# Sums of a Strassen product's weight quarters: accumulating DMAs that read SBUF in place of HBM, with other buffer counts and another place for a part of the adaLN sums

## The chip, the cores and the metric

The kernel runs on one core of a Trainium2 chip. The metric is device time in microseconds (us) of one execution; lower is better. The kernel before takes 841.71 us, the median of 3 runs (840.68 to 843.01).

## What is computed

A trunk of two layers on 512 tokens of width 1024, in float32. In each layer:

```
mod = silu(c) @ w_ada + b_ada                # shift, scale, gate: the three adaLN thirds
h   = rms_norm(x) * (1 + scale) + shift
x_rg, z_rg, x_ml, z_ml, o = split(h @ w_in)  # five parts of 1024 columns
y_rg = rglru(conv(x_rg)) * silu(z_rg)        # gates by block-diagonal products, then a scan over tokens
y_ml = mlstm(x_ml, o) * silu(z_ml)           # 4 heads of 256, in chunks of 128 tokens
x   = x + gate * (concat(y_rg, y_ml) @ w_out)
```

Then a last RMS norm. What the change touches is the part of `h @ w_in` that gives `o` and `z_ml`, called **oz** here, and the adaLN sums.

## The kernel before

**Precision.** A float32 product is done as three matmuls of a rounded format: each operand is split into a high and a low part, and TensorE adds high*high, low*high and high*low (`mm3`, recorded at L154). A weight tile comes in by one DMA of 512 KB into a buffer of the kind `raw`; ScalarE (ACT) casts it to `whi` (L184) and VectorE (DVE) forms `wlo = raw - whi` (L191). That pair of instructions is called a split here. A pair stays until the last matmul that reads it; the raw buffer is free once both have read it, unless somebody else still wants it.

**The planner.** The program is first recorded by a planner, as operations with an engine, a guessed cost, and the tiles they read and write. The planner then fixes the order of each engine's instructions, with due times counted from TensorE's order, and gives every tile a numbered buffer of its kind's pool (`kinds`). Engines run their lists in order and wait for one another by semaphores. So buffer counts and guessed costs change the order everywhere, also in stages that the source does not touch. Loads are issued by SP (L233); an accumulating DMA (`out += source`) is issued by GpSimd (POOL, L241), and is one of the instructions that it issues in order.

**Stages of a layer.** Layer 0: the start and the norm; the mLSTM heads' inputs, to 150 us; the oz stage, from 150 to 238; the RG-LRU stage, from 238 to 341; the out product (two passes, out and outq), from 341. Layer 1's oz stage begins at 537, its RG-LRU stage at 642, and its out product at 744. Boundaries overlap, since the planner mixes neighbours.

**oz.** For a head, `ml_oz` (L1006 on) computes o and z for 512 tokens by a Strassen-like scheme of 7 products in place of 8. Activations are cut in quarters (two halves of the width, two halves of the tokens), and the head's weights in quarters q0, q1, q2, q3 (width half by the columns of o or z), each 512 KB. The products, with the activation quarter or sum of quarters and the weight that they use:

| product | activations | weights |
|---|---|---|
| h11 | quarter | q0 |
| s1 | sum | q0 + q1 |
| s2 | sum | q0 + q1 + q3 |
| h12 | quarter | q2 |
| s3 | sum | q1 + q3 |
| h22 | quarter | q0 + q1 + q3 + q2 |
| s4 | sum | q3 |

Each product is 24 matmuls of 256 columns (4 pieces of width, 2 of tokens, 3 of precision). The weight sums grow in place: one raw buffer `ta` holds q0, is split for h11, gets q1 added by a DMA, is split for s1, gets q3, is split for s2, gets q2, is split for h22. A second one, `tb`, holds q1 and gets q3 for s3. An addition to `ta` can start only when the split before it has read the buffer. Before the change every addition reads its quarter from HBM, and s4 and h12 load theirs plainly: four plain loads and four accumulating ones in a head, 512 KB each.

Around a head's products stand, on TensorE, those of the attention part (`ml_sw`, `ml_sv`, `ml_yt`); its outputs are named `num`, `Mbc`, `yT`. `mrs` is a small power (an inverse root) on GpSimd that `ml_yt` needs; `vh` are small memsets there.

**adaLN sums.** `mod_units` yields one unit at a time: a load of 512 KB of `w_ada2` into a raw buffer by SP, and two DVE operations that multiply by silu(c) and add into `macc` (L199; the first pair at L208). A third is 8 units. A layer's loop has a generator `bg` of 24 units in layer 0 and 8 in layer 1 (`MODAT`). `step_mod(bg, n)` takes n of them. Before, two are taken in each of the four heads, and the rest, two per step, in the out product, which uses the gate third first.

**RG-LRU stage.** `rg_x`, `rg_gates`, `rg_z` are products of 512 columns (rgx, pa, px, rgz), with many DVE operations on their results (`rconv`, `ti`, `tr`, `om`, `rzt`).

Of the kernel before, what the change touches and what calls it, by code (L numbers as in the profile page):

```python
# [15 lines left out]
ALU = mybir.AluOpType  # L16
# [92 lines left out]
class Planner:  # L109
# [128 lines left out]

    def qdma(self, out, in_, nbytes):

        self.op("POOL", lambda: self.nc.gpsimd.dma_start(out.ap(), in_, accum_op=ALU.add), [out], [out], 1.0,  # L241
                tail=nbytes)

    def lat(self, a, b):
        if a != b:
# [191 lines left out]
def trunk_kernel(ctx: ExitStack, tc: tile.TileContext, x, cT, params, bif, bgate, fg,  # L437
# [6 lines left out]
    def pools(name, n, **kw):  # L444
        return n, [ctx.enter_context(tc.tile_pool(name=f"{name}{i}", bufs=1, **kw)) for i in range(n)]

    kinds = {
        "heap": pools("heap", 66),
        "raw": pools("raw", 4),
        "whi": pools("whi", 5),  # L450
        "wlo": pools("wlo", 4),
        "gate": pools("gate", 1),
        "gpart": pools("gpart", 2),
# [8 lines left out]
    def slot(name, dt=F32, shape=(128, 512)):  # L462
        return P.tile("heap", shape, dt, name)

    def bank(name, shape=(128, 512)):
        return P.tile("ps", shape, F32, name)
# [29 lines left out]
    def load_w(src, shape, raw=None, pieces=1):  # L496
        raw = raw or load_raw(src, shape, pieces)
        hi = P.tile("whi", (128,) + shape, F32R, "whi")
        lo = P.tile("wlo", (128,) + shape, F32R, "wlo")
        n = shape[0] // pieces  # L500
        for k in range(0, shape[0], n):
            split(hi[:, k:k + n], lo[:, k:k + n], raw[:, k:k + n])
        return hi, lo

    def mm3(ps, lh, ll, rh, rl, start, stop):
        P.mm(ps, lh, rh, start, False)
        P.mm(ps, lh, rl, False, False)
        P.mm(ps, ll, rh, False, stop)
# [172 lines left out]
    def step_mod(bg, n):  # L681
        for _ in range(n):
            next(bg, None)
# [80 lines left out]
    def chan_group(l, g, hT, names):  # L764
        ps = [bank(n) for n in names]
        for kh in range(2):
            u = w_in_unit(l, g, kh)
            for cc in range(2):
                for k in range(4):
                    chan_mm(ps[cc], u, hT, kh, k, cc, ALLT, kh == 0 and k == 0, kh == 1 and k == 3)  # L770
        return ps
# [10 lines left out]
    def silu2(ps, name, shape=(128, 512)):  # L782

        th = slot(name + "t", F32, shape)
        P.act(th, ps, AF.Tanh, scale=0.5)
        P.stt(th, th, 1.0, ps, ALU.add, ALU.mult)
        return th
# [208 lines left out]
    def ml_oz(l, h, hT, st):  # L996

        src = w_oz[l, h].rearrange("u p (k w n) -> p u k w n", k=2, w=2)  # L1000
        q = [src[:, :, k, w, :] for k in range(2) for w in range(2)]
        form = [[(hT[2 * p + k][0][:, ts], hT[2 * p + k][1][:, ts]) for p in range(4)]
                for k, ts in ((0, slice(0, 256)), (1, slice(0, 256)), (1, slice(256, 512)))]
        h11, h12, h22 = form
        s1, s2, s3, s4 = [[st["sf"][p][n] for p in range(4)] for n in range(4)]

        def parts(raw):
            return load_w(None, (4, 256), raw)

        def quarter(src):  # L1010
            raw = P.tile("raw", (128, 4, 256), F32, "raw")
            P.dma(raw, src, 1 << 19)
            return raw

        def add(raw, src):
            P.qdma(raw, src, 1 << 19)

        def product(f, w):
            ps = bank("oz", (128, 2, 256))
            for b in range(2):  # L1020
                bs = slice(128 * b, 128 * b + 128)
                for k in range(4):
                    mm3(ps[:, b, :], f[k][0][:, bs], f[k][1][:, bs], w[0][:, k, :], w[1][:, k, :],
                        b == 0 and k == 0, b == 1 and k == 3)
            return ps

        def wide(name):
            return slot(name, F32, (128, 2, 256))

        ta = quarter(q[0])  # L1030
        ps = product(h11, parts(ta))
        p1 = wide("ozp")
        P.acopy(p1, ps)
        add(ta, q[1])
        p5 = product(s1, parts(ta))
        c12, c22 = wide("ozc"), wide("ozc")
        P.acopy(c22, p5)
        add(ta, q[3])
        ps = product(s2, parts(ta))
        u = wide("ozu")  # L1040
        P.tt(u, ps, p1, ALU.add)
        P.tt(c12, c22, u, ALU.subtract)
        ps = product(h12, parts(quarter(q[2])))
        o = [wide("oz") for _ in range(2)]
        z = [wide("oz") for _ in range(2)]
        P.tt(p1, ps, p1, ALU.add)
        P.act(o[0], p1, AF.Tanh, scale=0.5)
        yield
        tb = quarter(q[1])
        add(tb, q[3])  # L1050
        ps = product(s3, parts(tb))
        P.tt(u, ps, u, ALU.add)
        P.tt(c22, c22, u, ALU.subtract)
        add(ta, q[2])
        ps = product(h22, parts(ta))
        P.tt(u, ps, u, ALU.add)
        P.act(o[1], u, AF.Tanh, scale=0.5)
        ps = product(s4, parts(quarter(q[3])))
        P.tt(c12, ps, c12, ALU.add)
        for n, c in ((1, c22), (0, c12)):  # L1060
            P.act(z[n], c, AF.Tanh, scale=0.5)
            P.stt(z[n], z[n], 1.0, c, ALU.add, ALU.mult)
        st["oz"][h] = (o, z)
        yield
# [85 lines left out]
    def rg_gates(l, g, st):  # L1150
        if g % 2 == 0:
            st["wr"] = load_w(w_rg[l, g // 2], (4, 2, 128))
            st["om"] = [slot("om") for _ in range(4)]
        wr, om = st["wr"], st["om"]
        for cc in range(2):
            r = 2 * g + cc
            n = r % 4
            xr, hi, lo = st["xr"].pop(r)
            pa, px = bank("pa"), bank("px")
            mm3(pa, wr[0][:, n, 0, :], wr[1][:, n, 0, :], hi, lo, True, True)  # L1160
            mm3(px, wr[0][:, n, 1, :], wr[1][:, n, 1, :], hi, lo, True, True)


            tr, q = slot("tr"), slot("q")
            P.ts(q, pa, par[:, l, P_BA + r:P_BA + r + 1], ALU.add, 0.0, ALU.min)
            P.act(tr, pa, AF.Tanh, scale=0.5, bias=hb[:, l, r:r + 1])
            P.act(q, q, AF.Exp)
            P.act(tr, tr, AF.Abs)
            P.stt(tr, tr, 1.0, q, ALU.add, ALU.mult)
            P.act(q, tr, AF.Exp, scale=hsp[:, l, r:r + 1])  # L1170
            P.act(q, q, AF.Square)
            P.act(tr, tr, AF.Tanh, scale=sp4[:, l, r:r + 1])
            P.act(om[n], q, AF.Square)
            P.stt(om[n], om[n], 1.0, tr, ALU.add, ALU.mult)
            ti = slot("ti")
            P.act(ti, px, AF.Tanh, scale=0.5, bias=hb[:, l, 8 + r:9 + r])
            P.stt(ti, ti, 1.0, xr, ALU.add, ALU.mult)
            st["ai"][r] = (q, ti)

    def rg_z(l, g, hT, st):  # L1180
        pz = chan_group(l, 4 + g, hT, ("rgz0", "rgz1"))
        for cc in range(2):
            st["rz"][2 * g + cc] = silu2(pz[cc], "rz")

    def rg_tail(l, bt, st):
        om = st["om"]
        P.slack = SL_TAIL
        for n in range(4):
            P.act(om[n], om[n], AF.Sqrt, extra=0.7)
        for n in range(4):  # L1190
            r = 4 * bt + n
            a, u = st["ai"].pop(r)
            P.tt(u, u, om[n], ALU.mult)
            P.scan(u, a, u, ALU.mult, ALU.add)
            P.tt(u, u, st["rz"].pop(r), ALU.mult)
            hi, lo = slot("yh", F32R), slot("yl", F32R)
            split_scaled(hi, lo, u, 0.25)
            st["y"][r] = (hi, lo)
        P.slack = SL
# [85 lines left out]
    for l in range(L):  # L1285
# [68 lines left out]
        bg = itertools.chain(*[mod_units(*j) for j in MODAT[l]])  # L1354
        for h in range(NH):
            oz = ml_oz(l, h, hT, st)
            next(oz)
            step_mod(bg, 1)
            if h:
                ml_sv(l, h - 1, st)  # L1360
            else:
                next(gates)
                ml_sw(0, st)
            next(oz)
            step_mod(bg, 1)
            if h + 1 < NH:
                ml_sw(h + 1, st)
            if h:
                ml_yt(l, h - 1, st)
# [3 lines left out]
        ml_yt(l, 3, st)  # L1373
        rg_gates(l, 0, st)
        rg_z(l, 0, hT, st)
        rg_gates(l, 1, st)
        rg_z(l, 1, hT, st)
        rg_tail(l, 0, st)
        rg_x(l, 2, hT, st)
        rg_x(l, 3, hT, st)  # L1380
        rg_gates(l, 2, st)
        rg_z(l, 2, hT, st)
        rg_gates(l, 3, st)
        rg_z(l, 3, hT, st)
        rg_tail(l, 1, st)
        xt = load_x(x if l == 0 else x1d)
        def during_first(u):
# [105 lines left out]
```

## Time and profile before

| what | us |
|---|---|
| median of 3 runs | 841.71 |
| lowest, highest | 840.68, 843.01 |
| the profiled execution's own time | 843.48 |
| its span in the profile | 841.8 |
| granted TensorE clock, mean | 0.99 |

The profile names the engines PE (TensorE matmul), PEld (its weight load), DVE (VectorE), ACT (ScalarE), POOL (GpSimd) and SP. A `q` behind a name is the engine's sequencer, or its DMA issues. L154 and so on are lines of the kernel before. In a row `raw<-in_w_oz_dram`, the tile is written from an input in HBM; numbers in tile names (`raw_2843`) count the recorded tiles, and differ between the two programs. A window row gives for each engine busy time and, in brackets, the count of instructions that began in it. The queue q0 (software_dynamic) holds the accumulating DMAs alone, and q1 the plain ones. A wait row says which engine waited, at which output, for whom, and for how long in all, how many times, and the longest. The chain follows the last instruction back to what released it.

### The profile page before, as it was taken

Reading aid. Unit: us, or ns where it says so; the run is one execution under the profiler, and the core shown is the slowest. Engines: PE = TensorE matmul, PEld = TensorE weight load, DVE = VectorE, ACT = ScalarE, POOL = GpSimd, SP = SyncE. Lnnn points to the kernel's source line nnn. Section 1 sums busy time; section 2 is a strip of 40 time slices with the busy share of each in tenths; the row PEclk is TensorE's granted clock in tenths of the full one; section 3 lists DMA queues with packets and bytes.
Section 4 is the critical chain, followed back from the end, with each engine's and each line's share of the span. In section 5 each row is a group of like instructions: output and inputs, shape, how many; then the busy total and the mean of one; then the engine's idle time right before and its main releaser. Section 6 shows DMA issues by size and latency. Waiting matters only on the chain.

```text
span 841.8 us, 14032 instructions
## 1 busy us (share of the span) xinstructions
PE 814.7 (97%) x5222; PEld 724.9 (86%) x5222; DVE 679.6 (81%) x1339; ACT 530.0 (63%) x1045; POOL 80.4 (10%) x96
## 2 busy tenths in 40 slices
PE   4999999998899999999999999999989999999996
PEld 3778899998888888889999789999988888888996
DVE  5598957897999899788569887589999988976552
ACT  4378755765667879921347667657676687894222
POOL 3000012222011000000010001212120100000000
PEclk9999999998999999999999999999999999999999
DMA  9933346867753414668632443467984442373202
GB/s 317 355 140 125 77 93 132 177 143 170 189 157 120 138 62 147 216 218 269 212 95 101 151 115 61 76 153 174 225 181 146 148 127 76 100 250 100 76 1 100
DMA packets 66243, 124.46 MB, mean 148 GB/s; under 512 B 4864, under 2 KB 39680, under 8 KB 66176
## 3 DMA queue, kind: packets, MB, share of 16 engines
q1 hardware_dynamic: 49280, 106.80, 38.4%
q0 software_dynamic: 16896, 16.78, 13.3%
q8 instruction: 41, 0.67, 0.3%
q14 instruction: 26, 0.21, 0.1%
HBM read 119.36 MB, written 4.19 MB: 147 GB/s over the span
## 4 chain that ended last, share of the span: by engine, by line
PE 85%; DVE 5%; DMA 4%; issue 2%; ACT 2%; POOL 0%; SPq 0%; POOLq 0%; DVEq 0%; ACTq 0%
PE oz L154 12%; PE mx L154 11%; PE rgx L154 11%; PE out L154 11%; PE rgz L154 11%; PE outq L154 10%; PE S L154 3%; DMA raw<-in_w_oz_dram 3%; PE v L154 3%; PE p L154 2%; PE num L154 2%; PE A L154 2%; DVE wlo L191 2%; PE px L154 1%; PE pa L154 1%
## 5 line engine op out<-in xcount | busy, mean ns | idle before, releaser
L184 ACT CAST whi<-raw 128x1024 fp32r<-128x1024 f32 (+1 forms) x157 | 156.5, 1007 | 121.0 <-DMA raw<-in_w_out_dram 35.0
L191 DVE TENSOR_TENSOR wlo<-raw,whi 128x1024 fp32r<-128x1024 f32 (+1 forms) x157 | 180.7, 1160 | 45.6 <-PE outq L154 12.0
L154 PE MATMUL oz<-whi,sh 128*128 128x256 f32 x256 | 74.4, 291 | 4.9 <-ACT ozp L184 3.6
L154 PE MATMUL oz<-wlo,sh 128*128 128x256 f32 x256 | 73.9, 289 | 0.7 <-DVE wlo L191 0.7
L154 PE MATMUL oz<-whi,sl 128*128 128x256 f32 x256 | 73.7, 288 | 0.0
L154 PE MATMUL outq<-whi,yh 128*128 128x256 f32 x256 | 71.4, 283 | 0.0
L154 PE MATMUL outq<-wlo,yh 128*128 128x256 f32 x256 | 71.4, 283 | 0.0
L154 PE MATMUL outq<-whi,yl 128*128 128x256 f32 x256 | 71.3, 282 | 0.0
L241 POOL DMA_DIRECT2D raw<-in_w_oz_dram x32 | 41.4, 1337 | 296.2 <-DVE wlo L191 93.9
L154 PE MATMUL mx<-hh,whi 128*128 128x512 f32 (+1 forms) x166 | 59.5, 359 | 2.1 <-ACT whi L184 2.1
L154 PE MATMUL mx<-hl,whi 128*128 128x512 f32 (+1 forms) x166 | 58.4, 352 | 0.1
L154 PE MATMUL oz<-wlo,hh 128*128 128x256 f32 x192 | 55.2, 288 | 2.7 <-DVE wlo L191 2.7
L154 PE MATMUL mx<-hh,wlo 128*128 128x512 f32 (+1 forms) x166 | 57.5, 349 | 0.0
L154 PE MATMUL oz<-whi,hh 128*128 128x256 f32 x192 | 55.3, 288 | 0.0
L154 PEld LDWEIGHTS oz<-whi,sh 128*128 128x128 f32 x256 | 50.1, 196 | 5.6 <-ACT ozp L184 4.1
L154 PE MATMUL oz<-whi,hl 128*128 128x256 f32 x192 | 54.8, 286 | 0.0
L154 PEld LDWEIGHTS oz<-wlo,sh 128*128 128x128 f32 x256 | 50.0, 195 | 1.0 <-DVE wlo L191 0.9
L154 PE MATMUL rgx<-hl,whi 128*128 128x512 f32 x128 | 50.8, 397 | 0.0
L154 PE MATMUL rgx<-hh,whi 128*128 128x512 f32 x128 | 50.7, 396 | 0.0
L154 PE MATMUL rgx<-hh,wlo 128*128 128x512 f32 x128 | 50.5, 395 | 0.0
L154 PE MATMUL out<-whi,yh 128*128 128x512 f32 x128 | 50.5, 395 | 0.0
L154 PE MATMUL rgz<-hh,whi 128*128 128x512 f32 x128 | 50.5, 394 | 0.0
(279 smaller groups left out, 2460.6 us busy)
## 6 DMA issues: line engine op xcount, KB each, us to landing
raw<-in_w_in_dram SPq DMA_DIRECT2D x45, 512.0 KB, 3.5
raw<-in_w_oz_dram SPq DMA_DIRECT2D x32, 512.0 KB, 4.7
raw<-in_w_oz_dram POOLq DMA_DIRECT2D x32, 512.0 KB, 6.1
raw<-in_w_ada_dram SPq DMA_DIRECT2D x32, 512.0 KB, 4.4
raw<-in_w_out_dram SPq DMA_DIRECT2D x32, 512.0 KB, 4.1
wada<-in_w_adb_dram SPq DMA_DIRECT2D x24, 256.0 KB, 5.3
x<-in_x_dram SPq DMA_DIRECT2D x16, 256.0 KB, 5.4
raw<-in_w_qk_dram SPq DMA_DIRECT2D x8, 512.0 KB, 3.5
```

The costliest lines, as they stand in the source:

```text
L154: self.nc.tensor.matmul(out.ap(), lhsT=lhsT.ap(), rhs=rhs.ap(), start=start, stop=stop, **kw)
L184: self.op("ACT", lambda: self.nc.scalar.copy(out.ap(), in_.ap()), [out], [in_], 0.1 + 0.00084 * in_.n)
L191: self.op(eng, lambda: e.tensor_tensor(out=out.ap(), in0=a.ap(), in1=b.ap(), op=op), [out], [a, b], c)
L241: self.op("POOL", lambda: self.nc.gpsimd.dma_start(out.ap(), in_, accum_op=ALU.add), [out], [out], 1.0, tail=nbytes)
```

## The change

In `ml_oz`, each quarter is loaded once by SP and stays in its raw buffer: `ta` (q0), `tb` (q1), `td` (q3), `tc` (q2). The four additions of a head become SBUF to SBUF: ta += tb, ta += td, tb += td, ta += tc. So a head has four plain loads as before, and four accumulating DMAs that no longer read HBM. The source of an addition is now a tile, and so an input that the planner must keep, and wait for; the planner's guess for such an instruction goes from 1.0 to 1.3. For two raw buffers more there is one whi less and two heap buffers less. The eight units of the adaLN sums that stood in the heads now stand in the RG-LRU stage, two behind each `rg_z`.

```diff
@@ qdma @@
-        self.op("POOL", lambda: self.nc.gpsimd.dma_start(out.ap(), in_, accum_op=ALU.add), [out], [out], 1.0,
-                tail=nbytes)
+        self.op("POOL", lambda: self.nc.gpsimd.dma_start(out.ap(), in_.ap(), accum_op=ALU.add), [out], [out, in_],
+                1.3, tail=nbytes)
@@ kinds @@
-        "heap": pools("heap", 66),
-        "raw": pools("raw", 4),
-        "whi": pools("whi", 5),
+        "heap": pools("heap", 64),
+        "raw": pools("raw", 6),
+        "whi": pools("whi", 4),
         "wlo": pools("wlo", 4),
@@ ml_oz @@
-        add(ta, q[1])
+        tb = quarter(q[1])
+        add(ta, tb)
         p5 = product(s1, parts(ta))
...
-        add(ta, q[3])
+        td = quarter(q[3])
+        add(ta, td)
         ps = product(s2, parts(ta))
...
-        ps = product(h12, parts(quarter(q[2])))
+        tc = quarter(q[2])
+        ps = product(h12, parts(tc))
...
-        tb = quarter(q[1])
-        add(tb, q[3])
+        add(tb, td)
         ps = product(s3, parts(tb))
...
-        add(ta, q[2])
+        add(ta, tc)
         ps = product(h22, parts(ta))
...
-        ps = product(s4, parts(quarter(q[3])))
+        ps = product(s4, parts(td))
@@ the loop over heads, and the RG-LRU stage behind it @@
             next(oz)
-            step_mod(bg, 1)
...
             next(oz)
-            step_mod(bg, 1)
...
         rg_z(l, 0, hT, st)
+        step_mod(bg, 2)
         rg_gates(l, 1, st)
         rg_z(l, 1, hT, st)
+        step_mod(bg, 2)
...
         rg_z(l, 2, hT, st)
+        step_mod(bg, 2)
         rg_gates(l, 3, st)
         rg_z(l, 3, hT, st)
+        step_mod(bg, 2)
```

How the instructions then stand, at two places. First GpSimd's list for the additions of layer 0's fourth head. Before, `raw_2843` is its ta and `raw_3041` its tb:

```order
L241 DMA raw_2843<-in_w_oz_dram 128x4x256 [waits DMAHW5_49,DMAHW7_49,DMAHW2_49,DVE_49]
L241 DMA raw_3041<-in_w_oz_dram 128x4x256 [waits DMAHW4_49,DMAHW7_49,DMASW2_49,DVE_49]
L241 DMA raw_2843<-in_w_oz_dram 128x4x256 [waits DMASW4_49,DVE_49]
L191 TENSOR_TENSOR mrs_3157<-mms_3134,mhalf_429 128x2 [waits DVE_49]
L191 TENSOR_TENSOR mrs_3173<-mms_3137,mhalf_429 128x2 [waits DVE_49]
L1096 MEMSET vh_3211 128x2x2
L1096 MEMSET vh_3234 128x2x2 [waits DVE_49,PE_49]
L241 DMA raw_2843<-in_w_oz_dram 128x4x256 [waits DMASW6_49,DVE_49]
```

And after, where `raw_2580` is ta, `raw_2622` tb, `raw_2933` td and `raw_2964` tc:

```order
L241 DMA raw_2580<-raw_2622 128x1024 [waits DMAHW1_49,DMAHW2_49,DMASW5_49,DVE_49]
L241 DMA raw_2622<-raw_2933 128x1024 [waits DMAHW3_49,DMASW7_49,DMASW4_49]
L241 DMA raw_2580<-raw_2933 128x1024 [waits DVE_49]
L191 TENSOR_TENSOR mrs_3111<-mms_3085,mhalf_426 128x2 [waits DVE_49]
L191 TENSOR_TENSOR mrs_3126<-mms_3097,mhalf_426 128x2 [waits DVE_49]
L1098 MEMSET vh_3165 128x2x2 [waits PE_49,Activation_49]
L1098 MEMSET vh_3202 128x2x2 [waits DVE_49]
L241 DMA raw_2580<-raw_2964 128x1024 [waits DMAHW4_49,DMASW6_49,DVE_49]
```

The order of the four is the same. What changed are the sources, the shape of a transfer (rows of 1024 elements in place of four pieces of 256), and the waits: the second addition, to tb, now waits for the first one too, which reads tb (`DMASW` is an accumulating DMA, `DMAHW` a plain one).

Second, VectorE's list in layer 0's RG-LRU stage. Before:

```order
L191 TENSOR_TENSOR wlo_4042<-raw_3943,whi_4031 128x1024
L199 SCALAR_TENSOR_TENSOR ti_4045<-ti_4045,rconv_3840 128x512
L199 SCALAR_TENSOR_TENSOR tr_3972<-tr_3972,q_3989 128x512
L199 SCALAR_TENSOR_TENSOR tr_4038<-tr_4038,q_4016 128x512
L199 SCALAR_TENSOR_TENSOR rzt_4078<-rzt_4078,rgz0_3991 128x512
L191 TENSOR_TENSOR wlo_4090<-raw_3951,whi_4059 128x1024
```

And after, about the same place:

```order
L191 TENSOR_TENSOR wlo_4044<-raw_3769,whi_4027 128x1024
L191 TENSOR_TENSOR ti_3846<-ti_3846,rzt_3921 128x512
L199 SCALAR_TENSOR_TENSOR macc_3904<-raw_4012,csil_562,macc_3904 128x512
L199 SCALAR_TENSOR_TENSOR om_4052<-om_4052,tr_3975 128x512
L199 SCALAR_TENSOR_TENSOR macc_3916<-raw_4012,csil_562,macc_3916 128x512
L199 SCALAR_TENSOR_TENSOR om_4068<-om_4068,tr_3970 128x512
L191 TENSOR_TENSOR wlo_4086<-raw_3780,whi_4074 128x1024
```

The two sums of a unit (`macc`) now stand between the splits and the RG-LRU's own operations. On SP, the adaLN loads are gone from between the loads of oz and stand among those of the RG-LRU stage.

## The prediction

> **What bounds the kernel now.** I read the page's busy times and chain first, then windows over the stages, then TensorE's waits, the chain and the DMA inside the windows that lose time.
>
> The page's span, its busy times and the chain by engine:
>
> ```profile
> span 841.8 us, 14032 instructions
> PE 814.7 (97%) x5222; PEld 724.9 (86%) x5222; DVE 679.6 (81%) x1339; ACT 530.0 (63%) x1045; POOL 80.4 (10%) x96
> PE 85%; DVE 5%; DMA 4%; issue 2%; ACT 2%; POOL 0%; SPq 0%; POOLq 0%; DVEq 0%; ACTq 0%
> ```
>
> TensorE (PE) is the bound: 97% busy, and 85% of the chain. A change in DMAs can win only what PE loses, by waiting or by running at a lower granted clock. Windows over the oz stages of layer 0 (150 to 238) and layer 1 (from 537) show where that is; the columns are length, busy time with instructions of PE, PEld, DVE, ACT and POOL, granted clock, DMA share and GB/s:
>
> ```profile
> 150.00:180.00 30.00, 30.00 (x251) 29.70 (x250) 27.83 (x62) 22.81 (x54) 6.16 (x7) 1.00 0.80 171
> 180.00:198.00 18.00, 14.40 (x107) 14.13 (x106) 14.96 (x26) 12.04 (x23) 3.95 (x4) 0.88 0.90 185
> 198.00:212.00 14.00, 14.00 (x111) 13.95 (x110) 11.02 (x32) 7.23 (x20) 4.04 (x5) 0.92 0.58 141
> 212.00:222.00 10.00, 7.27 (x49) 7.07 (x48) 10.00 (x17) 6.36 (x11) 1.44 (x2) 0.83 0.64 159
> 537.00:590.00 53.00, 52.90 (x440) 51.67 (x439) 46.83 (x111) 35.84 (x79) 13.81 (x12) 1.00 0.67 150
> 590.00:612.00 22.00, 21.67 (x180) 21.24 (x179) 21.00 (x45) 14.36 (x30) 5.31 (x6) 1.00 0.96 219
> 612.00:626.00 14.00, 11.77 (x83) 11.20 (x82) 13.92 (x26) 11.09 (x23) 3.14 (x7) 0.88 0.88 171
> ```
>
> At full pace PE does 251 instructions in 30 us, 0.1195 us each. From 180 to 222 it did 267, worth 31.9 us, in 42: 10.1 us lost, 6.3 of them idle (3.60 and 2.73), the rest at a clock of 0.83 to 0.92. From 590 to 626 it did 263, worth 31.4, in 36: 4.6 lost. So **at most about 14.7 us can come back**.
>
> What PE waited for between 150 and 238 (total, times, longest), and then the chain there (start, length, what):
>
> ```profile
> PE oz L154 <- ACT ozp L184: 3.6, 1, 3.6
> PE oz L154 <- DVE wlo L191: 2.7, 1, 2.7
> ```
>
> ```profile
> 175.65 4.96 issue
> 180.63 1.30 POOL raw L241
> 181.97 10.66 DMA raw<-in_w_oz_dram
> ...
> 193.65 0.59 ACT ozp L184
> 194.28 1.86 PE oz L154 x7
> ```
>
> The wait put down to an ACT copy ends an accumulating load that took 10.66 us. The issues of the accumulating loads over the whole run, their landing times, and the two queues and the issues of 150 to 238 (packets, MB, share of 16 engines; count, size, median us to landing):
>
> ```profile
> L241 POOL DMA_DIRECT2D raw<-in_w_oz_dram x32: 1264/1280/1826, 87.2 to 620.2; - x32
>   DMA to landing us min/median/max: 5.7/6.1/10.7
> ```
>
> ```profile
> q0 software_dynamic: 5643, 5.60, 42.2%
> q1 hardware_dynamic: 5664, 9.44, 32.7%
> ...
> raw<-in_w_oz_dram POOLq DMA_DIRECT2D x9, 512.0 KB, 6.5
> raw<-in_w_oz_dram SPq DMA_DIRECT2D x8, 512.0 KB, 5.6
> raw<-in_w_ada_dram SPq DMA_DIRECT2D x7, 512.0 KB, 4.6
> ```
>
> 10.66 us is the longest landing of 32, against a shortest of 5.7. The price of one transfer of 512 KB (0.524 MB), in time of all 16 DMA engines: an add 42.2% x 88 us / (5.60 / 0.524) = 3.47 us, a plain load 32.7% x 88 / (9.44 / 0.524) = 1.60 us.
>
> A head of oz is, in PE's order, 168 matmuls of seven products and 38 other instructions: 206 x 0.1195 = 24.6 us. Before, it needs four adds, four loads and two adaLN loads of DMA: 4 x 3.47 + 6 x 1.60 = 23.5 us. That is 96% of 24.6: little room, so an add lands late when others share its time.
>
> **The change part by part.** *The adds.* Their number stays 32, their source is now a tile in SBUF. No row shows such a transfer. As cheap as a plain load it takes 1.6 us of all engines; as dear as three plain streams (two read, one written) 4.8. I take two streams, 3.2, since that is nearest to the 3.47 of the same add with its source in HBM. The adaLN loads leave the heads, so a head needs 4 x 3.2 + 4 x 1.6 = 19.2 us, 78% of 24.6; with the ends, 12.8 (52%) and 25.6 (104%). The Trainium skill ("DMA: Bandwidth & Descriptors", section "Issuing engines are not separate DMA queues") speaks against the change's first part: transfers from whatever queue run on the same 16 engines and interleave. By that, an add kept at 3.47 leaves 20.3 us a head, all of the relief being the adaLN loads'; the trace agrees that the queues share (q0 and q1 together, 42.2 + 32.7%, beside the late landings).
>
> *How late an add may land.* GpSimd issues in order: the last add of a head (ta+=tc) stands ahead of the first of the next head (ta+=tb). A weight tile is then split by ACT and DVE:
>
> ```profile
> L184 ACT CAST whi<-raw x157: 391/1052/1150, 14.3 to 806.9; 128x1024 fp32r<-128x1024 f32 x145, 128x256 fp32r<-128x256 f32 x12
> L191 DVE TENSOR_TENSOR wlo<-raw,whi x157: 416/1221/1229, 15.4 to 812.4; 128x1024 fp32r<-128x1024 f32 x145, 128x256 fp32r<-128x256 f32 x12
> ```
>
> A split is 1.05 + 1.22 = 2.3 us. From s2's split in one head to s2's split in the next: issue 1.3, add 6.1, split 2.3, add 6.1, split 2.3, 18.1 us, 6.5 less than PE's 24.6. Two landings like the 10.66 (2 x 4.6 = 9.2 more) make it 27.3 and PE waits; landings at the median leave it no wait. So the loss follows the late landings, and those the load on the DMA. As a rough estimate the waiting in a shared queue of load u goes as u/(1-u): 0.96 gives 24, 0.78 gives 3.5, which would leave about a seventh of the loss. I keep a fifth, 3 us, for new waits of this order (below). This term is **-11.7 us**.
>
> *DVE in the heads.* Rows of the adaLN sums, by instruction and in the windows of both oz stages and both RG-LRU stages:
>
> ```profile
> L199 DVE SCALAR_TENSOR_TENSOR macc<-raw,csil,macc x56: 733/748/758, 179.4 to 667.6; 128x512 f32<-128x512 f32 x56
> 150.00:238.00 88.00, 0.00 (x0) 0.00 (x0) 7.21 (x11) 0.00 (x0) 0.94 0.75 172
> 537.00:642.00 105.00, 0.00 (x0) 0.00 (x0) 8.31 (x12) 0.00 (x0) 0.98 0.75 171
> 238.00:341.00 103.00, 0.00 (x0) 0.00 (x0) 3.96 (x6) 0.00 (x0) 1.00 0.41 132
> 642.00:744.00 102.00, 0.00 (x0) 0.00 (x0) 2.88 (x4) 0.00 (x0) 1.00 0.42 134
> ```
>
> A head loses two units of two operations, 4 x 0.748 = 3.0 us of DVE. DVE was full from 212 to 222 (10.00 of 10) and from 612 to 626 (13.92 of 14) while PE waited for a wlo split, so this helps the same 14.7 us; it is not a second sum.
>
> *The waits of the new order.* tb+=td waits for two loads and for ta+=tb to have landed, since tb is its source; behind it on GpSimd stand ta+=td, two small powers (mrs) that ml_yt's matmuls need, memsets and ta+=tc. Cost if tb+=td is late: s2's split. It has the 6.5 us above, and td is loaded a head ahead with six raws. I take 0, bounds 0 to 6 a layer, that is, up to the whole return. One whi buffer less: a cast can run ahead by one tile less, at most 1.05 us a head; wlo had four before and bounds the split anyway. 0, bounds 0 to 4 a layer.
>
> *The RG-LRU stage* gets 16 sums (of the 8 units) in place of 6 and 4:
>
> ```profile
> 238.00:341.00 103.00, 103.00 (x465) 84.27 (x464) 94.83 (x146) 83.91 (x134) 3.01 (x2) 1.00 0.41 132
> 341.00:387.00 46.00, 46.00 (x202) 37.27 (x201) 38.68 (x53) 22.90 (x31) 0.00 (x0) 1.00 0.64 212
> 642.00:744.00 102.00, 102.00 (x460) 83.31 (x459) 93.08 (x144) 82.62 (x132) 3.07 (x2) 1.00 0.42 134
> ```
>
> DVE becomes 94.83 + 10 x 0.748 = 102.3 of 103, and 93.08 + 12 x 0.748 = 102.1 of 102: full. PE has no wait there now, DVE's splits run ahead of it, by up to three tiles, and what it fails to finish falls into the out stage, where it has 46 - 38.68 = 7.3 us free. I take 0. The cover gone, the sums would cost 10 x 0.748 = 7.5 in one layer and 9.0 in the other. The 8 loads, 8 x 1.6 = 12.8 us, fit a DMA busy 41%.
>
> *Start.* With six raws two more loads of w_in stand ahead of the first adaLN weights, 2 x 1.6 = 3.2 us on a DMA busy 0.99:
>
> ```profile
> 15.00:45.00 30.00, 29.93 (x230) 22.79 (x234) 18.32 (x61) 10.67 (x26) 1.25 (x2) 1.00 0.99 353
> PE modps L154 <- DVE ms L208: 6.8, 1, 6.8
> ```
>
> The second row is from TensorE's waits over the whole run: modps, the first user of those weights, waited 6.8 us for DVE, not for them. I take 0, bounds 0 to 3.2. Two heap buffers less, and layer change and tail: 0.
>
> Sum on the profiled execution (843.5: span 841.8 and 1.7 around it): 843.5 - 11.7 = 831.8. That execution is 1.8 over the median 841.7, so the median goes to **830**.
>
> **The rivals.**
>
> *B, cheap adds.* They take 1.6 us and land like the adaLN loads (4.6). The loop is 18.1 - 3.0 = 15.1, a head's DMA 12.8; all 14.7 come back: 827. For it: the packets become four times longer (rows of 4 KB for 1 KB). Against: the 3.47 row. The Trainium skill ("DMA: Bandwidth & Descriptors", section "Anatomy of one DMA — SWDGE (gpsimd) path") has a fit of about 2 us and the bytes at 436 GB/s, 3.2 us to landing here as an estimate by that page; the trace's shortest, 5.7 with its source in HBM, disagrees.
>
> *C, the relief does not reach PE.* The late wait was the order on GpSimd (4.96 us of "issue" ahead of the add), not the DMA; tb+=td, which now waits for another add, sits in the same place and hands the wait on. Then 840 to 842.
>
> *D, slower: the adds are dear.* At 4.8 us a head needs 25.6 of 24.6, saturated. The old loss stays, and each of eight heads is at least 1 us late: 843.5 + 8 - 1.8 = 850. It decides from 24.6, where an add costs (24.6 - 6.4) / 4 = 4.55. For it: an add already costs 2.2 times a load with one stream in SBUF. Against: it no longer reads HBM.
>
> *E, DVE bounds the RG-LRU stage.* It gives back 7.5 to 9.0 a layer at most; with half of that, 8 in both, 838; with all 16.5, 847.
>
> What a wait costs beside itself: the granted clock was 0.83 in the 10 us around the 2.73 us wait, and 0.88 and 0.92 at and after the 3.60 us one; so 6.3 us of waits cost 10.1, and I count any wait that stays at 1.6 of itself (10.1 / 6.3): the 3 us kept above are some 1.9 us of waits. The Trainium skill ("TensorE: Matmul & The Clock Gate", section "Part 1: The HAM clock gate") halves the clock after an idle window of about 3.4 us; by that rule the 2.7 us wait would have cost itself alone, and the trace disagrees.
>
> **How the numbers follow.** Forecast 0.49 (830), B 0.17 (827), C 0.11 (841), D 0.14 (850), E 0.09 (838 to 847). About 0.3%, 2.5 us, is what a measurement here can tell from no change. Faster: 0.48 + B 0.17 + 0.02 of C + 0.03 of E = 0.70. Same: 0.01 + 0.08 + 0.05 of E = 0.14. Slower: D 0.14, 0.01 of C, 0.01 of E = 0.16. The range goes from 824 (B and the spread of the runs) to 845 (C and most of E), leaving out D and the ends of E, about 0.18. The forecast's own range is 827 to 834.
>
> **What would show it.** Right: in the heads, landings of the adds at 4.5 to 6.5 us with no 10; the 3.6 and 2.7 us waits gone; q0's share of the oz windows below 40%; clock 1.00 from 180 to 222; layer 0's oz stage about 8 us shorter, layer 1's 4; the RG-LRU stages as long as before with DVE above 97%. Wrong: adds landing at 8 us and more, or GpSimd standing at tb+=td while PE waits for s2's weights (D, C), PE waits on wlo in the RG-LRU stage (E), or modps waiting for its load.

## The result and the profile after

The kernel after takes 828.2 us (median of 4 runs, 827.94 to 828.32), the one before 842.17 (4 runs): a ratio of 0.9836, 95% interval 0.9819 to 0.9853, 14 us less. The profiled execution took 827.94 us, its span 826.0; before it was 843.48 and 841.8.

The page of after: span, busy times, the chain by engine.

```profile
span 826.0 us, 14051 instructions
PE 807.3 (98%) x5222; PEld 718.8 (87%) x5222; DVE 676.5 (82%) x1339; ACT 536.2 (65%) x1049; POOL 66.0 (8%) x96
PE 96%; ACT 1%; DMA 1%; DVE 1%; issue 0%; SPq 0%; POOLq 0%; ACTq 0%
```

The chain was 85% TensorE and is 96% now; VectorE's share of it went from 5% to 1% and DMA's from 4% to 1%. The windows of the heads of layer 0 and of the two RG-LRU stages (length, PE, PEld, DVE, ACT, POOL, clock, DMA share, GB/s):

```profile
150.00:180.00 30.00, 30.00 (x249) 29.57 (x248) 27.69 (x63) 25.10 (x58) 5.00 (x8) 1.00 0.66 154
180.00:198.00 18.00, 18.00 (x154) 18.00 (x153) 17.47 (x37) 13.42 (x26) 2.69 (x4) 1.00 0.68 160
198.00:212.00 14.00, 14.00 (x120) 13.96 (x119) 13.74 (x29) 11.51 (x26) 4.20 (x6) 1.00 0.52 113
212.00:222.00 10.00, 10.00 (x87) 10.00 (x86) 9.87 (x26) 9.09 (x19) 1.50 (x3) 1.00 0.74 200
228.00:331.00 103.00, 103.00 (x465) 84.23 (x464) 97.78 (x153) 85.34 (x133) 2.00 (x2) 1.00 0.40 133
626.00:728.00 102.00, 102.00 (x461) 83.37 (x460) 96.77 (x152) 84.38 (x132) 1.99 (x2) 1.00 0.40 133
```

From 180 to 222 TensorE did 361 instructions where it did 267, never idle, at clock 1.00. VectorE is at 97 to 99% there (17.47 of 18, 13.74 of 14, 9.87 of 10), and at 95% in the RG-LRU stages, which TensorE walks through as fast as before. Between 150 and 230 no wait of TensorE is left; over the whole run these are the longest:

```profile
PE modps L154 <- DMA wada<-in_w_ada_dram: 9.4, 2, 8.1
PE mx L154 <- ACT whi L184: 2.2, 1, 2.2
```

And the additions: their issue on GpSimd, their landing, the queue's share of the DMA over the span.

```profile
L241 POOL DMA_DIRECT2D raw<-raw x32: 841/854/1043, 106.3 to 607.2; - x32
...
DMA to landing us min/median/max: 4.5/5.3/9.2
```

```profile
q1 hardware_dynamic: 49280, 106.80, 38.2%
q0 software_dynamic: 4608, 16.78, 11.5%
```

An addition takes 11.5% x 826.0 / 32 = 2.97 us of all 16 engines (before, by 13.3% of 841.8: 3.50). One still lands after 9.2 us, and nobody on TensorE waits for it. The prediction had named landings of 8 us and more as a sign of being wrong, so this is a first hint that late landings were not the whole story.

### The profile page after: what moved, and what is told of

It is laid out like the page before. It is cut to its first block, busy times and chain, and to the rows that moved or that the text cites. A ratio compares the mean times of both kernels' runs of the same rounds, so it can differ in the third digit from the quotient of the medians.

```text
span 826.0 us, 14051 instructions
## 1 busy us (share of the span) xinstructions
PE 807.3 (98%) x5222; PEld 718.8 (87%) x5222; DVE 676.5 (82%) x1339; ACT 536.2 (65%) x1049; POOL 66.0 (8%) x96
## 3 DMA queue, kind: packets, MB, share of 16 engines
q0 software_dynamic: 4608, 16.78, 11.5%
## 4 chain that ended last, share of the span: by engine, by line
PE 96%; ACT 1%; DMA 1%; DVE 1%; issue 0%; SPq 0%; POOLq 0%; ACTq 0%
PE oz L154 18%; PE mx L154 11%; PE outq L154 11%; PE rgx L154 11%; PE out L154 11%; PE rgz L154 11%; PE S L154 4%; PE num L154 3%; PE v L154 3%; PE p L154 3%; PE A L154 2%; PE px L154 1%; PE pa L154 1%; DMA x<-in_x_dram 1%; PE hT L163 1%; PE modps L154 1%
## 5 line engine op out<-in xcount | busy, mean ns | idle before, releaser
L154 PE MATMUL oz<-wlo,sh 128*128 128x256 f32 x256 | 72.1, 282 | 0.0
L241 POOL DMA_DIRECT2D raw<-raw x32 | 27.7, 865 | 294.5 <-DVE wlo L191 127.8
L154 PE MATMUL rgz<-hh,wlo 128*128 128x512 f32 x128 | 50.5, 395 | 0.0
L154 PE MATMUL out<-whi,yl 128*128 128x512 f32 x128 | 50.5, 394 | 0.0
```

The lines of the kernel that those rows point to most:

```text
L154: self.nc.tensor.matmul(out.ap(), lhsT=lhsT.ap(), rhs=rhs.ap(), start=start, stop=stop, **kw)
```

## The experiments

Three theories stood at the start. Theory 1 is the prediction's: the DMA had too little room in the heads, so additions landed late. Theory 2: four raw buffers were too few, so loads were issued late. Theory 3: VectorE had too little time in the heads, and the 3.0 us of adaLN sums a head were the loss. Each run has its own times of the kernel before, taken on the same chip; runs are compared by their ratios to these.

### Taking the change apart

e1_sums_in_heads is after with the last two hunks of the diff undone (`step_mod(bg, 1)` twice in each head, none behind `rg_z`).

> The kernel after, with the adaLN units back in the heads (two a head, as before the change). Theory 1 (the loss was late additions on a DMA with too little room): a head's DMA is 4 x 2.94 + 6 x 1.63 = 21.5 us of 24.6, 88%, against 96% before; about a third of the 14.7 us comes back as waits, 832 to 834. Theory 2 (the two raw buffers more, which let loads be issued earlier, are the gain): no change from after, 828 to 829. Theory 3 (the 3.0 us of VectorE time a head were the loss): nearly all is lost again, 838 to 842.

Measured: 836.52 us, 0.9923 (0.9901 to 0.9945). Between what theories 1 and 3 had said. TensorE waits here for VectorE, half of it at a place that no DMA feeds (`num` needs `vl`, the low part of v, in `ml_sv`):

```profile
PE num L154 <- DVE vl L191: 1.6, 2, 0.8
PE oz L154 <- DVE wlo L191: 1.6, 3, 0.6
```

e2_only_sums_moved is before with those two hunks alone.

> The kernel before, with only the adaLN units moved to the RG-LRU stage; additions from HBM, 4 raw buffers. Theory 1: a head's DMA is 4 x 3.47 + 4 x 1.63 = 20.4 us of 24.6, 83%; a fifth of the loss stays, 829 to 832. Theory 2: the raw buffers are as few as before, but two of them a head less are asked for by adaLN; most of the loss stays, 836 to 841. Theory 3: all comes back, 827 to 829.

Measured: 829.96 us, 0.9847 (0.9821 to 0.9874). Not to be told from after (0.9836): the move of the sums by itself gives the gain, as far as the times can tell. Theory 2 in its plain form falls: four raw buffers are enough here.

e3_only_buffers is before with the three counts alone:

```diff
-        "heap": pools("heap", 66),
-        "raw": pools("raw", 4),
-        "whi": pools("whi", 5),
+        "heap": pools("heap", 64),
+        "raw": pools("raw", 6),
+        "whi": pools("whi", 4),
```

> The kernel before, with only the buffer counts of after (6 raw, 4 whi, 64 heap); additions from HBM, adaLN units in the heads. Theory 1: DMA as full as before (23.5 of 24.6 us), 838 to 842. Theory 2: 828 to 831. Theory 3: 840 to 843.

Measured: 844.56 us, 1.0013 (0.9998 to 1.0028). No gain. TensorE's longest wait in the heads is no longer for a split, but for `vl` again:

```profile
PE num L154 <- DVE vl L191: 6.6, 2, 3.3
```

In layer 0, the chain to that wait begins with an addition that lands after 9.76 us (from 173.84) and then runs through VectorE's list, two adaLN sums of 1.32 us among it.

e4_after_with_hbm_adds is the sum of the two: before with the counts and with the sums moved; that is, after with its additions from HBM.

> The kernel after, with the additions from HBM as before (6 raw buffers, adaLN units in the RG-LRU stage). Theory 1: as e2_only_sums_moved, 829 to 832, additions at about 3.47 us of all DMA engines. Theory 2 and theory 3: 828 to 829.

Measured: 835.32 us, 0.9906 (0.9878 to 0.9933), worse than all had said. The wait of TensorE, and the chain that leads to it in layer 0:

```profile
PE yT L163 <- DVE mfac L199: 4.6, 2, 2.5
```

```profile
188.45 11.08 DMA raw<-in_w_oz_dram
...
199.61 0.29 ACT whi L184
...
200.56 2.09 ACT junk L177 x8
...
202.68 0.30 DVE mms L208
...
206.04 0.08 DVE mfac L199
...
206.19 0.41 PE yT L163 x2
```

And GpSimd at that time:

```profile
202.99 2.27 POOL L191 TENSOR_TENSOR mrs<-mms,mhalf 128x2 f32<-128x2 f32 x2
```

An addition lands after 11.08 us. ScalarE's cast of that tile stands in ScalarE's list ahead of eight small operations (`junk`) that the mean squares `mms` need; GpSimd's powers `mrs` start as soon as `mms` is there, `mfac` needs them, and `ml_yt` needs `mfac`. So a late landing does reach TensorE here, by way of ScalarE's order. In layer 1 the same chain begins with a landing of 11.53 us. Is that the price of transfers from HBM, or of the order that the planner made for this program?

### Place and length of the source

e7_hbm_4kb_rows and e8_hbm_1kb_rows keep what after records for the planner, and so its order on every engine; only the DMA that is sent out has another source.

```diff
-        self.op("POOL", lambda: self.nc.gpsimd.dma_start(out.ap(), in_.ap(), accum_op=ALU.add), [out], [out, in_],
+        self.op("POOL", lambda: self.nc.gpsimd.dma_start(out.ap(), hbm, accum_op=ALU.add), [out], [out, in_],
...
# e8: hbm is the quarter itself, rows of 256 elements
-        add(ta, tb)
+        add(ta, tb, q[1])
# e7: hbm is always this, rows of 1024 elements
+            w_ada2[0, 0].rearrange("p (k n) -> p k n", k=4)
```

> The kernel after with its own order on every engine, but each addition reads HBM in rows of 4 KB (of another weight, so the sums are wrong). If the place of the source makes an addition dear: 3.5 us of all engines an addition as before, 0.988 to 0.992. If the length of the rows does: 2.9 us and 0.983 to 0.986. If the loss of e4_after_with_hbm_adds (0.991) came from the order that the planner made for it: 0.983 to 0.986 too, and then e8_hbm_1kb_rows as well.

> The kernel after with its own order on every engine, but each addition reads its quarter from HBM, in rows of 1 KB as before the change. Place or row length of the source: 3.5 us an addition, 0.988 to 0.992. The order that the planner made for e4: 0.983 to 0.986.

Measured: e7 827.37 us, 0.9807 (0.9778 to 0.9837); e8 828.87 us, 0.9823 (0.9787 to 0.9858). Both are as fast as after. So, in after's order, the source in SBUF, the change's name-giving part, is worth nothing that these runs can tell. And e4 lost by its order: e8 sends the same transfers as e4. The additions of e7, then those of e8:

```profile
L241 POOL DMA_DIRECT2D raw<-in_w_ada_dram x32: 844/860/1231, 105.9 to 606.8; - x32
...
DMA to landing us min/median/max: 5.3/5.6/10.3
```

```profile
L241 POOL DMA_DIRECT2D raw<-in_w_oz_dram x32: 1264/1279/1856, 106.9 to 609.0; - x32
...
DMA to landing us min/median/max: 5.7/6.1/11.5
```

An 11.5 us landing, longer than any of before, costs e8 nothing; in e4's order TensorE waits 4.6 us behind landings of that length.

### DMA or VectorE in the heads

e5_loads_in_heads and e6_vector_in_heads put one half each of the adaLN units back into the heads of after:

```diff
# e5, at both places in a head
+            raw = load_raw(w_ada2[0, 0], (2, 512))
+            P.ts(sm("dmy", (1,)), raw[:, 0, 0:1], csil[:, 0:1], ALU.mult)
# e6, at both places in a head
+            for _ in range(2):
+                P.stt(dmy, st["o"][n], csil[:, 0:1], dmy, ALU.mult, ALU.add)
```

> The kernel after, with two more plain loads of 512 KB a head (their data go unused but for one column, in a tiny VectorE operation): the DMA half of the adaLN units is back in the heads, the VectorE half is not. After stood at 0.984 of before, e1_sums_in_heads with both halves at 0.992. Theory 1 (DMA room): 21.5 us of DMA a head in place of 18.3, most of the loss of e1 returns, 0.989 to 0.993. Theory 3 (VectorE time): no loss, 0.983 to 0.986.

> The kernel after, with four more VectorE operations of 512 columns a head (3.0 us, their result unused), gated by the head's own o, and no load: the VectorE half of the adaLN units is back in the heads, the DMA half is not. Theory 1: 0.983 to 0.986. Theory 3: most of the loss of e1 returns, 0.989 to 0.993.

Measured: e5 827.83 us, 0.9815 (0.9785 to 0.9845); e6 843.48 us, 1.0003 (0.9988 to 1.0019). 1 MB more of loads a head costs nothing; 16 more VectorE operations a layer take the whole gain back. Theory 1, that the load on the DMA makes the loss, fails in e5 and e8. (No run has the dear additions and the adaLN loads together in after's order.) But e6 and e1 also have orders of their own, so one more run puts the VectorE operations into after's order: e11_after_more_vector.

```diff
         P.tt(c12, c22, u, ALU.subtract)
+        # and behind P.tt(c22, c22, u, ALU.subtract): sent out with it, twice
+        nc.vector.scalar_tensor_tensor(out=dmy, in0=dmy, scalar=csil[:, 0:1].ap(), in1=dmy, op0=ALU.mult, op1=ALU.add)
```

> The kernel after with its own order on every engine, and four more VectorE operations of 512 columns a head (on a scratch tile) put behind the two subtractions for c12 and c22; no load. Theory 3: VectorE's need in the heads goes from 96 to 108%, 2 us a head over what TensorE takes, 6 to 16 us in both layers, 0.991 to 1.003 of before, with waits of oz and num for VectorE. Theory 1: 0.983 to 0.986. The order alone (theory 4: e6 lost by the order that was made for it): 0.983 to 0.987.

Measured: 848.3 us, 1.0057 (1.0042 to 1.0073): 32 operations of about 0.75 us, 24 us in all, cost some 19. TensorE waits for VectorE again:

```profile
PE yT L163 <- DVE mfac L199: 8.9, 4, 2.3
PE modps L154 <- DVE ms L191: 6.9, 1, 6.9
PE cumb L154 <- DVE lf L199: 3.2, 2, 1.6
```

(modps is at the start, and waits 8 to 10 us in all kernels, for VectorE or for its load.) In layer 0's chain around 208, four of the added operations, 2.84 us, stand ahead of the `mfac` that `yT` waits for:

```profile
206.03 0.67 DVE dmy L1042
...
210.38 0.75 DVE dmy L1042
211.14 0.07 DVE mfac L199
```

How near VectorE is to its limit has to be read between two landmarks of TensorE, since a window of fixed time holds less of TensorE's work when TensorE waits, while VectorE runs on. The rows go from a layer's first oz matmul to its last one, in which TensorE has the same work in each of these kernels: here layer 0 of before, after, e11 and, for the next section, e9.

```profile
128.40:235.70 107.30, 100.78 (x803) 99.16 (x803) 93.37 (x212) 69.94 (x146) 26.20 (x27) 0.95 0.74 166
```

```profile
129.40:225.40 96.00, 95.89 (x804) 94.79 (x803) 89.07 (x205) 70.85 (x147) 19.79 (x26) 1.00 0.69 163
```

```profile
129.40:234.60 105.20, 98.11 (x804) 96.06 (x802) 97.52 (x216) 70.44 (x147) 19.36 (x26) 0.98 0.63 149
```

```profile
128.20:234.50 106.30, 100.74 (x804) 98.80 (x803) 89.98 (x213) 69.88 (x147) 26.24 (x27) 0.95 0.74 168
```

TensorE has 803 to 805 instructions there, worth 96 us at 0.1195 each. The length of the stage and VectorE's busy time in it, layer 0 and layer 1, in us:

| kernel | length | VectorE busy |
|---|---|---|
| before | 107.3, 101.5 | 93.4, 93.9 |
| after | 96.0, 96.1 | 89.1, 89.1 |
| e1 | 100.3, 100.2 | 93.2, 93.2 |
| e3 | 104.1, 105.6 | 94.4, 94.5 |
| e4 | 99.9, 100.6 | 89.2, 89.3 |
| e6 | 102.3, 104.1 | 94.6, 94.9 |
| e9 | 106.3, 101.3 | 90.0, 90.9 |
| e11 | 105.2, 103.9 | 97.5, 97.4 |

Only e11 asks more of VectorE than TensorE's 96 us. But long before that, what VectorE gets more to do lengthens the stage: from after to e1, e6 and e11 VectorE has about 4.1, 5.6 and 8.4 us a layer more, and the stage is about 4.2, 7 and 8.5 us longer. e1 and e6 have orders of their own; e11 has after's. VectorE's time is not all, either: e4 has after's VectorE time and a stage 4 us longer, and e3 has little more of it than e1 and a stage 4 to 5 us longer.

The 3.0 us a head, from which theory 3 reckons, are too many. Of the 16 sums of a layer's heads the planner leaves 10 in this stage, in before and in e1; of e6's 16 operations 10 stand there, and of e11's 14. Layer 0 of before, e6 and e11, VectorE's column:

```profile
128.40:235.70 107.30, 0.00 (x0) 0.00 (x0) 6.84 (x10) 0.00 (x0) 0.95 0.74 166
```

```profile
129.90:232.20 102.30, 7.40 (x10) 0.00 (x0) 1.00 0.62 153
```

```profile
129.40:234.60 105.20, 10.46 (x14) 0.98 0.63 149
```

So the change took 6.84 us, some 1.7 a head, and e11 gave more than that back.

### The same question asked of before

If VectorE's time were all, before without it should be as fast as after. e9_before_less_vector and e10_before_less_loads keep before's order and cut one half each of the units in the heads, but for a layer's first unit.

```diff
# e9: the sums of the gate third (w == 2), but for the first unit, on 8 columns of 512
                     P.stt(acc[hf], raw[:, hf, :], csil[:, k:k + 1], acc[hf], ALU.mult, ALU.add)
+                    if w == 2:
+                        def emit(a=acc[hf], r=raw[:, hf, :], s=csil[:, k:k + 1]):
+                            nc.vector.scalar_tensor_tensor(out=a.ap()[:, 0:8], in0=r.ap()[:, 0:8], scalar=s.ap(),
+                                                           in1=a.ap()[:, 0:8], op0=ALU.mult, op1=ALU.add)
+                        P.ops[-1].emit = emit
# e10: the loads, but for the first unit's, with 16 columns of 1024; the sums read acc in place of raw (not shown)
             raw = load_raw(w_ada2[MODJOBS.index((l, w)), k], (2, 512))
+            if w == 2 and k:
+                def emit(r=raw, s=w_ada2[MODJOBS.index((l, w)), k]):
+                    nc.sync.dma_start(r[:, 0, 0:16].ap(), s[:, 0:16])
+                P.ops[-1].emit = emit
```

> The kernel before with its own order on every engine; 14 of the 16 VectorE operations of the adaLN units in a layer's heads cut from 512 to 8 columns (so most of the gate third is left out), their loads kept. Theory 3 (VectorE time in the heads): about 2.4 us of it a head go, and 10 to 15 us of the loss, 0.982 to 0.988 of before. Theory 1 (DMA room): nothing goes, 0.996 to 1.002.

> The kernel before with its own order on every engine; 7 of the 8 adaLN loads in a layer's heads cut from 512 KB to 8 KB, the VectorE operations kept at 512 columns (on other data). Theory 1: a head's DMA falls from 23.5 to 20.7 us, and 8 to 12 us of the loss go, 0.985 to 0.990. Theory 3: 0.996 to 1.002.

Measured: e9 839.97 us, 0.9963 (0.9949 to 0.9978); e10 840.77 us, 0.9975 (0.9960 to 0.9991). Each gives 2 to 3 us. So both theories fail at the place where they should have paid: e9 comes out where theory 1 had it, and e10 where theory 3 had it. The chain around 180 us, in e9 and then in e10, is that of before:

```profile
175.47 4.92 issue
...
181.51 10.80 DMA raw<-in_w_oz_dram
```

```profile
175.89 4.90 issue
...
182.03 9.11 DMA raw<-in_w_oz_dram
```

So before's order holds something that neither half alone takes away. Before's GpSimd around there, SP's loads at 171.5 and 172.5 with their landings, and the DMA's use from 170 to 193 in 40 slices of 0.575 us:

```profile
170.90 1.35 POOL L241 DMA_DIRECT2D raw<-in_w_oz_dram  x1 [9.24 <-DVE wlo L191]
...
180.62 2.62 POOL L241 DMA_DIRECT2D raw<-in_w_oz_dram  x2 [4.98 <-issue]
```

```profile
L233 SPq DMA_DIRECT2D raw<-in_w_oz_dram x2: 378/378/378, 171.5 to 172.5; - x2
...
DMA to landing us min/median/max: 4.1/5.8/7.6
```

```profile
DMA  0000738979999999500000699999997999999999
```

The load at 172.5 is the third head's tb. It lands 7.6 us later, at 180.1; only then can GpSimd issue tb's addition, at 180.62, and ta's next addition, which stands behind it, at 181.97. The two then run side by side with a load and an adaLN load, and the second lands at 192.6. The DMA's row adds to this: it stood at 0 for the first 2.3 us and again for 2.9 us around 181, and at 9 nearly all the time behind that. It was held up, and then given all at once.

Why do these loads come so late? From 166 to 184 SP waited for raw buffers, among others for these two:

```profile
SPq L233 <- DVE macc L199: 9.4, 1, 9.4
...
SPq L233 <- DVE macc L208: 0.5, 1, 0.5
```

The tiles of the first two adaLN units, loaded at 158.93 and 163.79, held two of the four raw buffers until VectorE got to their sums. The load at 171.5 had waited 4.4 us for VectorE; tb's load, behind it, took the buffer that the first unit's sums (L208) left at 172.51; the load after that waited 9.4 us for the second unit's. e9 and e10 leave this as it is: the sums stand at the same places in VectorE's list, though short or on other data, and SP waits there 8.6 us in e9 and 9.2 in e10. So neither could take the late tb away.

After, in the same head, the first three additions go out 8 and 5 us apart (160.19, 168.07, 173.27), since tb had been loaded for another addition already; no adaLN unit holds a buffer there, and there are six:

```profile
160.19 0.84 POOL L241 DMA_DIRECT2D raw<-raw  x1 [1.49 <-DVE wlo L191]
...
168.07 0.85 POOL L241 DMA_DIRECT2D raw<-raw  x1 [3.14 <-DMA raw<-in_w_oz_dram]
173.27 0.84 POOL L241 DMA_DIRECT2D raw<-raw  x1 [4.34 <-DVE wlo L191]
```

In layer 1, e9's stage is hardly shorter than before's (101.3 and 101.5 us). There before's chain runs through VectorE from 600 to 619, with adaLN sums in it; in e9 they are short, and a landing of 9.73 us stands in the chain instead. Before, then e9:

```profile
614.78 1.41 DVE macc L199 x2
```

```profile
596.29 9.73 DMA raw<-in_w_oz_dram
```

What follows: that the adaLN units in the heads cost before its loss is shown by e2, which moves them and nothing else, and by e3, e7 and e8, where the buffer counts and the source do not give the gain. How they cost it is known in part. A unit takes VectorE time, and it holds a raw buffer. That VectorE's time in the heads costs about what it takes is shown in after's own order (e11, with one dose and at one place of the list). That held buffers make tb late, and two additions then land late, is read from the traces of before, e9 and e10; no run tries it alone. In before's order taking away nearly all of the sums' time (e9) or nearly all of the loads (e10) gives only 2 to 3 of 14 us; since before's order without both, and with its buffers free, was not tried, the shares of the two stay open. Open too is why e1 is 0.9% better than e3, both with six raw buffers and the sums in the heads: their additions differ in the source, which in after's order does not matter (e7, e8), and their orders differ; e3's order with e1's source was not tried.

### A mix of the counts

e12_raw5_whi5 is after with `pools("raw", 5)` and `pools("whi", 5)`, for the start, where TensorE's modps waits 8.1 us for a load.

> The kernel after with 5 raw buffers and 5 whi in place of 6 and 4. One w_in load less stands ahead of the first adaLN weights, 0.5 to 1.5 us less at the start; if five raw buffers still serve the heads, 0.981 to 0.984; if they don't, loads of oz come late and it is 0.986 to 0.992.

Measured: 828.64 us, 0.9827 (0.9808 to 0.9847), as after. The wait for that load is hardly shorter (7.7 us), so the one w_in load less does not show. Five raw buffers serve as well as six.

## Why the prediction was right, and where it was not

**The number.** 830 was forecast, 824 to 845 the range, and 828.2 came. The place was right: the loss was in the oz heads, and all that TensorE lost there came back. The bound of "at most about 14.7 us" was a little low, since its windows began at 180 and 590: the two oz stages became 11.3 and 5.4 us shorter (107.3 to 96.0, 101.5 to 96.1), and on the profiled executions 15.5 us came back. The 3 us kept for new waits were not needed. But the relief that the number was worked out from, that of the DMA, is not what the runs show, and to that extent the number came out right by luck.

**The step that failed** is "So the loss follows the late landings, and those the load on the DMA". e5 adds as much load to the DMA as the change took from the heads by the adaLN units, and nothing happens. e8 keeps the dear additions of 3.5 us and landings up to 11.5 us, and nothing happens. The load itself was set too high: the prediction reckons 23.5 us of DMA a head, but before's stage row has a DMA share of 0.74 over 107.3 us, 79 us for four heads, or 20 a head, against TensorE's 24. And the row of the DMA in the very stretch of the late landing shows it idle before. The u/(1-u) estimate had nothing under it. The first half of the step is true in some orders: in before, e4 and e9 a late landing does reach TensorE. What made it late in layer 0 of before was a late issue, behind raw buffers that adaLN units held.

**VectorE.** The prediction wrote that VectorE's relief "is not a second sum", and put it at 3.0 us a head. Its own rows show 7.21 and 8.31 us in its two windows, and in the stage it is 1.7 a head. VectorE's time does cost: in e1, e6 and e11 the stage grows by about what VectorE gets more to do, though its need stays below TensorE's 96 us in e1 and e6. In before, taking it away alone gave 3 us (e9), so no sum of its own can be given for it.

**The rivals.** B, cheap adds: the price fell from 3.50 to 2.97 us, below the 3.2 that was taken, but by the length of the rows (e7, from HBM: 11.9% x 825.6 / 32 = 3.07 us), and it doesn't move the time. C named the right place, the 4.96 us of "issue" on GpSimd ahead of the late addition, and expected the wait to be handed on; instead the change took its cause away, since tb's load no longer comes last. A landing whose wait is handed on to TensorE does show in e4, but by ScalarE's list. D is out: additions did not get dearer, and at 3.5 us they cost nothing in after's order (e8); 4.8 was not tried. E: VectorE in the RG-LRU stage reached 95%, not the 99% of the sum, in part since only 13 of the 16 sums (9.02 us in layer 0) fall into its window; from the first rgz matmul to the first one of the out product it takes 75.1 us as before (265.9 to 341.0, and 255.6 to 330.7).

**The start.** "I take 0, bounds 0 to 3.2": the first oz matmul starts at 129.4 in place of 128.4. Over all profiles it is at 128.2 to 129.1 with four raw buffers and at 128.9 to 129.9 with six: some 0.9 us, inside the bounds, taken as nothing. The sign that the prediction gave for being wrong here, modps waiting for its load, did come (8.1 us, where it had waited 6.8 us for VectorE before), at this small price.

## What to carry to other kernels

Before putting a wait down to the transfer that ended it, add up each engine's work between two landmarks of the engine that bounds the kernel, and not in a window of fixed time, where every wait of that engine makes the others look needier. A late landing can be a late issue: look at the issuing queue for what stands ahead, at the DMA's use just before, and at what freed the buffer that the transfer goes to. An experiment that takes away a thing's time may leave what the thing holds: e9 and e10 shorten the sums and the loads, and keep the raw buffers held as long. And where a planner orders the program, an edit's effect is its effect on the order too: e4 and e8 send the same transfers and differ by 0.8%.

## What the runs showed of the hardware

An accumulating DMA of 512 KB cost GpSimd 1.28 us to issue with rows of 1 KB (from HBM), and with rows of 4 KB 0.85 us from SBUF and 0.86 from HBM. It took 5.7 us at least to land from HBM in rows of 1 KB, 5.3 from HBM in rows of 4 KB, and 4.5 from SBUF in rows of 4 KB. In time of all 16 DMA engines it took 3.50, 3.07 and 2.97 us, where a plain load of 512 KB took 1.60.
